# The first y tile of an output projection: loaded into raw weight buffers, and its two casts put behind the last V strip's copies on ScalarE

## The chip, the core and the metric

The kernel runs on one core of a Trainium2 chip. The metric is device time in microseconds (us) of one execution, lower is better. Engines are named as the profile names them: PE (TensorE, matmuls), PEld (its weight loads), DVE (VectorE), ACT (ScalarE), POOL (GpSimd) and SPq (SyncE's queue, which issues all DMAs here).

## The reference

One encoder layer, applied to a prompt of 1024 tokens and a sample of 256, each with 16 meta tokens ahead, in float32:

```python
u = rms_norm(h, norm_w) @ w_in                      # 2048 -> 6656
qa, ka, va, za, qb, kb, vb, zb = split(u)
ya = global_gqa(rope(norm(qa)), rope(norm(ka)), va) * silu(za)          # 8 heads, 2 KV heads
yb = neighbourhood_attention(norm(qb), norm(kb), vb, rpb) * silu(zb)    # 8 heads, windows of 8 x 16
y = concat([ya, yb]) @ w_out
return h + y                                        # meta tokens dropped
```

## The kernel before

Activations lie transposed: model dimension on the 128 partitions, tokens along the free axis. Tokens are taken in two chunks (`chunk1`, `chunk2`). In each, the input projection runs strip by strip, a strip being 128 output columns (one head of Q, K, V or Z). `strips` (L192) walks the 2048 input dimensions in four chunks of four 128-row tiles (`WCH` = 4): it loads 256 KB of weights into a tile `wr` of the pool `raw` and calls `split` (L64). Nearly all large products are float32 done as three passes over a high and a low part: `split` has ScalarE cast a tile to the high part (L66) and VectorE subtract it to get the low part (L67). The three matmuls per tile are L227 to L229; results gather in the PSUM tiles `pp`, one of 512 tokens (operand `x`) and one of 272 (operand `xb`).

The pools that matter here: `raw` has 3 buffers in chunk 2, `w` has 4 buffers for high parts (tag `wh`) and 4 for low parts (tag `wl`). A raw buffer comes free when VectorE has made the low part from it, a wh or wl buffer only when TensorE has done the matmuls that read it.

Chunk 2 ends with the V strip of the last local head and then its Z strip (`self.turn` is set there: in each weight chunk the 272 tokens come first). A V strip is scaled by VectorE (`v_rows`, L289, tile `vt`), transposed by TensorE into the one PSUM tile of the pool `tp` (L540), and copied out by ScalarE (`rows_out`, L542 and L547, tile `vl`), from which it is stored. For the last V strip the transposes and the copies fall into the Z strip behind it: first a `tp` tile of 512 tokens, then one of 272, whose copies are an L542 of 128x256 and an L547 of 16x128.

Then comes the output projection (`outproj`, L1095): seven products of half matrices (numbered 1, 2, 5, 6, 7, 3, 4 in `order`, a scheme with seven instead of eight), each over 5 token tiles, for two column halves `b`. One such step is 24 matmuls (L1056, L1057, L1058: y high by w high, y high by w low, y low by w high, for k = 0 to 7). The very first step puts its result into the `tp` tile (`products`, `first`), so it can only begin when the last V copies have emptied that. Its operands are 16 weight tiles `wm` (`w_load`, `w_operand`; loaded into `ww` tiles that take over the buffers of `xb`, and split into `wm` tiles that take over those of `x`), and the y tile (1, 0) in two halves of four k each. `y_load` (L975) loads a half straight into a wl buffer, where VectorE makes the low part in place; `y_operand` (L989) casts the high part `yh`. Between the first steps stand pieces of the last local head's attention (`attend_strip`: scores L485, values L516 and L519 for four column strips), entered by a list of due work.

The order on each engine comes from a scheduler, with edges set by hand: `place_after` keeps an instruction behind another on the same engine. `behind_v` (L1034) puts a split's subtraction behind the last V scaling, and its cast behind one of the last two 512- or 256-wide V copies (`vlcopies`): behind the one but last, until more than 8 weight tiles have been made.

Of the kernel before, what the change touches and what calls it, by code (L numbers as in the profile page):

```python
# [12 lines left out]
F32 = mybir.dt.float32  # L13
F32R = mybir.dt.float32r
# [7 lines left out]
P = 128  # L22
# [26 lines left out]
WCH = 4  # L49
# [10 lines left out]
class Kern:  # L60
# [914 lines left out]
    def y_load(self, p, t):  # L975

        def half(i, h):
            r = self.yr.tile([P, 8, P], F32, tag="yr", name="yr")
            self.nc.sync.dma_start(r[:], self.yd[i][:, NT * h + t])
            return r[:]  # L980

        if p in (1, 2):
            los = [self.w.tile([P, WCH, P], F32R, tag="wl", name="yl") for _ in range(2)]
            for i, l in enumerate(los):
                self.lasty = self.nc.sync.dma_start(l[:].bitcast(F32), self.yd[p - 1][:, t, WCH * i:WCH * i + WCH]).ins
            return los
        return [half(*x) for x in {7: [(0, 0), (0, 1)], 5: [(0, 1), (1, 1)], 6: [(0, 0)], 3: [(1, 0)], 4: [(1, 1)]}[p]]

    def y_operand(self, p, t, r):  # L989
        nc = self.nc  # L990
        if p in (1, 2):
            his, los, full = [], r, [l[:].bitcast(F32) for l in r]
            for l, f in zip(los, full):
                his.append(self.w.tile([P, WCH, P], F32R, tag="wh", name="yh"))
                i = self.split(his[-1][:], l[:], f)
                if (p, t) == (1, 0):
                    self.behind_v(i)
            return his, los
        if p == 4:
            v = r[0]  # L1000
        elif p == 7:
            v = r[0]
            nc.vector.tensor_tensor(out=v, in0=v, in1=r[1], op=ALU.subtract)
        else:
            v = self.ysum[t][:]
            a, b, op = {5: (r[0], r[-1], ALU.add), 6: (v, r[0], ALU.subtract), 3: (r[0], v, ALU.subtract)}[p]
            nc.vector.tensor_tensor(out=v, in0=a, in1=b, op=op)
        his, los = [], []
        for i in range(2):
            his.append(self.w.tile([P, WCH, P], F32R, tag="wh", name="yh"))  # L1010
            los.append(self.w.tile([P, WCH, P], F32R, tag="wl", name="yl"))
            self.split(his[i][:], los[i][:], v[:, WCH * i:WCH * i + WCH])
        return his, los
# [318 lines left out]
```

## Time and profile before

| what | value |
|---|---|
| time, median of 3 runs | 2164.05 us (2163.06 to 2164.53) |
| span of the profiled execution | 2164.5 us, the same as the slowest run's time |
| TensorE busy | 2154.5 us |
| VectorE, ScalarE, GpSimd busy | 1654.7, 1187.6, 524.2 us |
| DMA queues' share of 16 engines | 53.7% |
| first matmul of the output projection | 1766.4 us |

In a time line each row is start, duration, engine, line, operation, output and input, and in brackets the idle time of that engine before the row and what ended it. A row with x4 holds four instructions, and its duration runs from the first's start to the last's end. Operations of one engine overlap a little, so the distance between two starts is shorter than one duration. A row of waits is: who, for whom, us in total, times, the longest. The granted clock is TensorE's, 1.00 being full speed.

### The profile page before, as it was taken

The page shows a single profiled execution, that of the slowest core. Times are in us where ns is not written, and L with a number is a line of the kernel's source. Part 1 is how long each engine was busy: PE and PEld are TensorE (multiplying, and loading weights), DVE is VectorE, ACT ScalarE, POOL GpSimd, SP SyncE. Part 2 cuts the span into 40 slices and gives each one's busy share as a digit, 9 for nine tenths or more (in the row PEclk, how much of TensorE's full clock was granted, in tenths as well). Part 3 has the DMA queues.
Part 4 walks back from the last instruction along what each step waited for, and adds up shares of the span by engine and source line. Part 5 has one row for each costly group of instructions (what it writes and reads, how often), then busy time and mean ns, then how long its engine had stood idle before and what let it go on. Part 6 is the DMA issues. An engine that isn't in the chain of part 4 may idle for free.

```text
span 2164.5 us, 33971 instructions
## 1 busy us (share of the span) xinstructions
PE 2154.5 (100%) x11745; PEld 1879.5 (87%) x11745; DVE 1654.7 (76%) x2989; ACT 1187.6 (55%) x2411; POOL 524.2 (24%) x250
## 2 busy tenths in 40 slices
PE   9999999999999999999999999999999999999999
PEld 7888888888888999999999999998999988888887
DVE  7698976788874899996798988778787766545763
ACT  7677644554565777776677775444444454232230
POOL 1142422222221223231133224333333311000000
PEclk9999999999999999999999999999999999999999
DMA  8667789988654333324233244644433354662663
GB/s 295 215 190 221 239 298 313 340 282 266 211 187 137 95 101 107 110 96 141 92 109 102 93 126 158 184 151 142 137 123 122 119 190 150 238 231 95 233 224 107
DMA packets 257420, 377.24 MB, mean 174 GB/s; under 512 B 43072, under 2 KB 108768, under 8 KB 257248
## 3 DMA queue, kind: packets, MB, share of 16 engines
q1 hardware_dynamic: 257248, 375.07, 53.7%
q8 instruction: 92, 1.51, 0.3%
q14 instruction: 80, 0.66, 0.1%
HBM read 281.01 MB, written 100.38 MB: 176 GB/s over the span
## 4 chain that ended last, share of the span: by engine, by line
PE 98%; DMA 1%; DVE 1%; SPq 0%; ACT 0%; issue 0%; DVEq 0%; ACTq 0%
PE pp L227 22%; PE pp L229 22%; PE pp L228 22%; PE pq L1056 6%; PE pq L1058 6%; PE pq L1057 6%; PE po L519 2%; PE sp L485 2%; PE sp L378 1%; PE sp L379 1%; PE sp L377 1%; PE po L420 1%; PE po L419 1%; PE po L418 1%; PE tp L540 0%; DMA yl<-yd 0%
## 5 line engine op out<-in xcount | busy, mean ns | idle before, releaser
L227 PE MATMUL pp<-x,wh 128*128 128x512 f32 (+1 forms) x1664 | 655.2, 395 | 0.9 <-ACT wh L66 0.6
L229 PE MATMUL pp<-x,wl 128*128 128x512 f32 (+1 forms) x1664 | 647.6, 390 | 0.0
L228 PE MATMUL pp<-x,wh 128*128 128x512 f32 (+1 forms) x1664 | 647.1, 389 | 0.0
L229 PEld LDWEIGHTS pp<-x,wl 128*128 128x128 f32 x1664 | 312.4, 188 | 60.9 <-DVE wl L67 0.2
L227 PEld LDWEIGHTS pp<-x,wh 128*128 128x128 f32 x1664 | 312.4, 188 | 59.2 <-ACT wh L66 2.8
L228 PEld LDWEIGHTS pp<-x,wh 128*128 128x128 f32 x1664 | 312.9, 188 | 52.0
L262 POOL PARTITION_ALL_REDUCE m<-ms x78 | 222.7, 2855 | 356.1 <-ACT ms L260 295.6
L67 DVE TENSOR_TENSOR wl<-wr,wh 128x512 fp32r<-128x512 f32 (+2 forms) x287 | 212.9, 743 | 121.8 <-ACT wh L66 88.8
L346 POOL PARTITION_ALL_REDUCE tot<-a x80 | 180.6, 2258 | 439.0 <-DVE a L343 408.4
L66 ACT CAST wh<-wr 128x512 fp32r<-128x512 f32 (+2 forms) x287 | 173.7, 611 | 183.6 <-PE pp L228 170.3
L228 PE MATMUL pp<-xb,wh 128*128 128x272 f32 x832 | 240.7, 289 | 0.0
L227 PE MATMUL pp<-xb,wh 128*128 128x272 f32 x832 | 239.8, 288 | 0.0
L229 PE MATMUL pp<-xb,wl 128*128 128x272 f32 x832 | 239.1, 287 | 0.0
L328 POOL PARTITION_ALL_REDUCE ma<-m x80 | 114.3, 1428 | 452.4 <-DVE m L326 443.7
L1056 PE MATMUL pq<-wm,yh 128*128 128x512 f32 x560 | 219.7, 392 | 3.8 <-ACT vl L547 3.8
L1057 PE MATMUL pq<-wm,yh 128*128 128x512 f32 x560 | 219.4, 392 | 0.0
L1058 PE MATMUL pq<-wm,yl 128*128 128x512 f32 x560 | 219.1, 391 | 0.0
L227 PEld LDWEIGHTS pp<-xb,wh 128*128 128x128 f32 x832 | 156.5, 188 | 7.5
L228 PEld LDWEIGHTS pp<-xb,wh 128*128 128x128 f32 x832 | 156.5, 188 | 7.5
L229 PEld LDWEIGHTS pp<-xb,wl 128*128 128x128 f32 x832 | 157.4, 189 | 0.3
L1056 PEld LDWEIGHTS pq<-wm,yh 128*128 128x128 f32 x560 | 105.8, 189 | 26.0 <-ACT vl L547 4.2
L1058 PEld LDWEIGHTS pq<-wm,yl 128*128 128x128 f32 x560 | 105.8, 189 | 22.2
(212 smaller groups left out, 3927.5 us busy)
## 6 DMA issues: line engine op xcount, KB each, us to landing
wr<-in_w_in SPq DMA_DIRECT2D x413, 256.0 KB, 3.5
wld<-wl SPq DMA_DIRECT2D x132, 256.0 KB, 4.2
wl<-wld SPq DMA_DIRECT2D x132, 256.0 KB, 3.1
yr<-yd SPq DMA_DIRECT2D x35, 512.0 KB, 5.0
wq<-in_w_out SPq DMA_DIRECT2D x64, 256.0 KB, 5.0
td<-wq SPq DMA_DIRECT2D x64, 256.0 KB, 4.4
ww<-td SPq DMA_DIRECT2D x64, 256.0 KB, 5.2
ww<-in_w_out SPq DMA_DIRECT2D x48, 256.0 KB, 5.1
```

The source lines that it names most:

```text
L66: self.hi = nc.scalar.copy(hi, full).ins
L67: return nc.vector.tensor_tensor(out=lo, in0=full, in1=hi.bitcast(F32), op=ALU.subtract).ins
L227: nc.tensor.matmul(p[:, :n], wh[:, k, :], xh[:, :n], start=first, stop=False)
L228: nc.tensor.matmul(p[:, :n], wh[:, k, :], xl[:, :n], start=False, stop=False)
L229: self.lastmm = nc.tensor.matmul(p[:, :n], wl[:, k, :], xh[:, :n], start=False, stop=last).ins
L262: nc.gpsimd.partition_all_reduce(m2[:], ms[:], P, RED.add)
L328: nc.gpsimd.partition_all_reduce(ma[:], m1[:], P, RED.max)
L346: nc.gpsimd.partition_all_reduce(tot[:], a1[:], P, RED.add)
L485: nc.tensor.matmul(dst, k[:, o:o + P], qfv[:, a:e, :], start=True, stop=True)
L1056: nc.tensor.matmul(ps, yh, wh, start=k == 0, stop=False)
L1057: nc.tensor.matmul(ps, yh, wl, start=False, stop=False)
L1058: self.lastmm = nc.tensor.matmul(ps, yl, wh, start=False, stop=k == 7).ins
```

## The change

The first y tile, (1, 0), is no longer loaded into wl buffers but as float32 into two buffers of the pool `raw` (tiles `yf`). `y_operand` then makes both parts in new wh and wl buffers, and places the cast of half n behind `vlcopies[n - 2]`: the first half's behind the copy of 512 tokens, the second's behind the last 256-wide copy. The other tiles keep the old way; `behind_v` is still used for weight tiles.

```diff
+        if (p, t) == (1, 0):
+            out = [self.raw.tile([P, WCH, P], F32, tag="raw", name="yf") for _ in range(2)]
+            for i, f in enumerate(out):
+                self.lasty = self.nc.sync.dma_start(f[:], self.yd[0][:, 0, WCH * i:WCH * i + WCH]).ins
+            return out
         if p in (1, 2):
             los = [self.w.tile([P, WCH, P], F32R, tag="wl", name="yl") for _ in range(2)]
...
     def y_operand(self, p, t, r):
         nc = self.nc
+        if (p, t) == (1, 0):
+            his, los = [], []
+            for n, f in enumerate(r):
+                his.append(self.w.tile([P, WCH, P], F32R, tag="wh", name="yh"))
+                los.append(self.w.tile([P, WCH, P], F32R, tag="wl", name="yl"))
+                i = self.split(his[n][:], los[n][:], f[:])
+                self.place_after(i, self.lastvt, "drain first")
+                self.place_after(self.hi, self.vlcopies[n - 2], "drain first")
+            return his, los
         if p in (1, 2):
             his, los, full = [], r, [l[:].bitcast(F32) for l in r]
             for l, f in zip(los, full):
                 his.append(self.w.tile([P, WCH, P], F32R, tag="wh", name="yh"))
-                i = self.split(his[-1][:], l[:], f)
-                if (p, t) == (1, 0):
-                    self.behind_v(i)
+                self.split(his[-1][:], l[:], f)
             return his, los
```

ScalarE at the end of the last Z strip, before (`vl` copies of V, `yh` casts of y, `wm` casts of projection weights):

```order
L542 COPY vl<-tp 128x512
L66 CAST yh<-yl 128x512
L66 CAST wm<-ww 128x512 x4
L66 CAST yh<-yl 128x512
L542 COPY vl<-tp 128x256
L547 COPY vl<-tp 16x128
L66 CAST wm<-ww 128x512 x4
```

The same place on ScalarE now:

```order
L542 COPY vl<-tp 128x512
L66 CAST yh<-yf 128x512
L66 CAST wm<-ww 128x512 x4
L542 COPY vl<-tp 128x256
L547 COPY vl<-tp 16x128
L66 CAST yh<-yf 128x512
L66 CAST wm<-ww 128x512 x4
L66 CAST yh<-yl 128x512
```

The second half's cast has gone from ahead of the last V copies to behind them, and a cast of tile (1, 1) has moved up behind the third group of weights.

VectorE at the same place, before (`yl` low parts of y, `wm` low parts of weights, `vt` and `z` the scaled last blocks of V and Z):

```order
L289 TENSOR_TENSOR vt<-pp,rb_320 128x272
L67 TENSOR_TENSOR yl<-yl,yh 128x512
L67 TENSOR_TENSOR wm<-ww,wm 128x512 x4
L67 TENSOR_TENSOR yl<-yl,yh 128x512
L302 TENSOR_TENSOR z<-pp,rb_320 128x272
L67 TENSOR_TENSOR wm<-ww,wm 128x512 x8
```

VectorE now:

```order
L289 TENSOR_TENSOR vt<-pp,rb_320 128x272
L67 TENSOR_TENSOR wm<-ww,wm 128x512 x4
L67 TENSOR_TENSOR yl<-yf,yh 128x512
L302 TENSOR_TENSOR z<-pp,rb_320 128x272
L67 TENSOR_TENSOR wm<-ww,wm 128x512 x4
L67 TENSOR_TENSOR yl<-yl,yh 128x512
L67 TENSOR_TENSOR yl<-yf,yh 128x512
L67 TENSOR_TENSOR wm<-ww,wm 128x512 x3
```

The first half's low part now stands behind the second four weights, and the second half's (the second `yl<-yf`) behind the third four and behind a low part of tile (1, 1). These two write wl buffers of the Z strip's third and fourth weight chunk; the loads of tile (1, 1) take those of the first and second.

SyncE now issues the two loads of `yf` on either side of a store (`q2d`, L283) and a load (`qfull`, L866) of the last local head, ahead of the projection's first weight loads; where the loads of tile (1, 0) stood among the weight loads, there now stand those of tile (1, 1). On TensorE the order differs only in the steps behind: the values of the last head's first strip (L516) stand behind 24 matmuls of the third step, where they stood behind those and 6 of the fourth.

## The prediction

> **What bounds the kernel now.** I read the page's busy times and the chain first, then TensorE's waits, then the time lines of the engines round the one wait that stands out.
>
> ```profile
> PE 2154.5 (100%) x11745; PEld 1879.5 (87%) x11745; DVE 1654.7 (76%) x2989; ACT 1187.6 (55%) x2411; POOL 524.2 (24%) x250
> PE 98%; DMA 1%; DVE 1%; SPq 0%; ACT 0%; issue 0%; DVEq 0%; ACTq 0%
> PE pq L1056 <- ACT vl L547: 3.8, 1, 3.8
> PE pp L227 <- ACT wh L66: 0.6, 1, 0.6
> ```
>
> TensorE is the bound: 2154.5 of 2164.5 us busy, and 98% of the chain. No edit on another engine pays except where TensorE waits, and it has one wait worth having: 3.8 us before the first product of the output projection (L1056). TensorE's time line at that place, then windows of the same trace (us of the stretch; busy time and count of PE, PEld, DVE, ACT, POOL; granted clock; DMA share; GB/s):
>
> ```profile
> 1762.19 0.39 PE L229 MATMUL pp<-x,wl 128*128 128x512 f32 x1
> 1766.38 0.79 PE L1056 MATMUL pq<-wm,yh 128*128 128x512 f32 x1 [3.80 <-ACT vl L547]
> 1774.84 0.60 PE L485 MATMUL sp<-qfull,kfull 128*128 128x128 f32 x4
> 1776.04 0.53 PE L1056 MATMUL pq<-wm,yh 128*128 128x512 f32 x1
> 1781.63 0.61 PE L485 MATMUL sp<-qfull,kfull 128*128 128x128 f32 x4
> ...
> 5.00:8.00 3.00, 2.48 (x9) 1.60 (x10) 2.45 (x6) 2.05 (x7) 0.00 (x0) 1.00 0.84 236
> 1762.50:1766.40 3.90, 0.10 (x2) 0.02 (x1) 0.46 (x1) 1.11 (x4) 0.00 (x0) 0.92 1.09 372
> 1766.40:1769.00 2.60, 2.60 (x6) 2.12 (x7) 2.60 (x6) 2.60 (x6) 0.00 (x0) 0.50 1.00 347
> 1769.00:1772.00 3.00, 3.00 (x8) 2.32 (x8) 3.00 (x6) 3.00 (x8) 0.00 (x0) 0.50 0.48 140
> ```
>
> The first product (24 matmuls) takes 1766.38 to 1774.84, 8.46 us; the second, the same 24, takes 1776.04 to 1781.63, 5.59 us, 0.23 a matmul. The windows say why: the granted clock is 0.50 for most of the first product. So the wait costs twice: without it the first product could start at 1762.19 + 0.23 = 1762.42; it starts 3.96 us later and then loses 8.46 - 5.5 = 2.96 us to the half clock. At most 6.9 us are to be had, 0.32%. (About 0.2%, 4.3 us, is what a measurement of this kernel can tell from no change.)
>
> Who holds TensorE? ScalarE (ACT), SyncE's queue (SPq) and VectorE (DVE) at that place:
>
> ```profile
> 1754.80 0.58 ACT L542 COPY vl<-tp 128x512 f32<-128x512 f32 x1
> 1758.49 0.62 ACT L66 CAST yh<-yl 128x512 fp32r<-128x512 f32 x1 [3.11 <-DMA yl<-yd]
> 1761.13 0.62 ACT L66 CAST wm<-ww 128x512 fp32r<-128x512 f32 x1 [0.34 <-DMA ww<-in_w_out]
> 1765.29 0.62 ACT L66 CAST yh<-yl 128x512 fp32r<-128x512 f32 x1 [3.53 <-DMA yl<-yd]
> 1765.81 0.36 ACT L542 COPY vl<-tp 128x256 f32<-128x256 f32 x1
> 1766.08 0.25 ACT L547 COPY vl<-tp 16x128 f32<-16x128 f32 x1
> ...
> 1754.37 0.33 SPq L1023 DMA_DIRECT2D ww<-in_w_out  x1
> 1754.79 0.38 SPq L985 DMA_DIRECT2D yl<-yd  x1
> 1759.47 0.33 SPq L985 DMA_DIRECT2D yl<-yd  x1
> ...
> 1753.66 2.49 DVE L67 TENSOR_TENSOR wm<-ww,wm 128x512 fp32r<-128x512 f32 x4
> 1761.79 0.69 DVE L67 TENSOR_TENSOR wm<-ww,wm 128x512 fp32r<-128x512 f32 x1 [0.15 <-ACT wm L66]
> 1766.55 0.43 DVE L302 TENSOR_TENSOR z<-pp,rb 128x272 f32<-128x272 f32 x1
> 1766.90 4.95 DVE L67 TENSOR_TENSOR wm<-ww,wm 128x512 fp32r<-128x512 f32 x8
> ```
>
> ScalarE stands 3.53 us before the second half of the first y tile, whose load was issued only at 1759.47; behind that cast wait the last V copies, which empty the PSUM tile (tp) that the first product needs. The load is late because its buffer is a wl buffer of the last strip and because SyncE issues it behind twelve weight loads.
>
> **The change part by part.** *The loads.* Each half now needs a raw buffer, freed when VectorE has split the last strip's second and third weight chunk:
>
> ```profile
> 1740.41 0.68 DVE L67 TENSOR_TENSOR wl<-wr,wh 128x512 fp32r<-128x512 f32 x1
> 1744.54 0.67 DVE L67 TENSOR_TENSOR wl<-wr,wh 128x512 fp32r<-128x512 f32 x1
> 1743.65 0.32 SPq L283 DMA_DIRECT2D q2d<-rs_r  x1
> 1746.55 0.32 SPq L866 DMA_DIRECT2D qfull<-q2d  x1
> 1750.04 1.05 ACT L66 CAST q<-qfull 128x1024 fp32r<-128x1024 f32 x1 [2.27 <-DMA vm<-vmd]
> ww<-in_w_out SPq DMA_DIRECT2D x16, 256.0 KB, 5.0
> ```
>
> The first load goes out at 1740.41 + 0.68 = 1741.1, ahead of a store that SyncE issues at 1743.65 anyway: free. The second stands behind qfull's load, at about 1746.9; even at the 5.0 us that a weight load of the same size takes to land, it is there by 1752. Both halves are in SBUF before ScalarE wants them (1754.80 + 0.58 = 1755.4). That takes the 3.11 and the 3.53 us out of ScalarE's queue. The price is one more issue and 256 KB in front of qfull's arrival and the first four weight loads: 262 kB at the 372 GB/s of the window above is 0.70 us. Those casts have some air, as VectorE starts its four wm subtractions at 1753.66 behind q's; but q's own cast (1750.04) can move too. The fifth weight load (1754.37) waits for the first of those subtractions, 1753.66 + 0.68, and everything behind it on SyncE follows. I call its delay s: 0 if the air covers it, 0.7 if nothing does; I take 0.3, since only q's load shares its arrival with the new one. The loads of tile (1,1) take the old places and bytes of tile (1,0)'s among the weight loads, so nothing else moves there.
>
> *ScalarE.* Ahead of the last V copies there now stand four wm casts and no y cast that can wait. The last of the four waited for its weights until 1761.13 before. It will again, to 1761.13 + s; behind a 512-wide cast the next operation starts 0.52 later (1765.29 to 1765.81), the next 0.27 later, and the last takes 0.25: the copies end at 1762.17 + s = 1762.5. TensorE could start at 1762.42. So the old wait is gone but for 0.1 us.
>
> *What is late next: VectorE.* The first half's yl now stands behind the four subtractions of wm: the fourth starts at 1761.79 + s = 1762.1, yl 0.61 later (the pitch in the row of eight: (4.95 - 0.69)/7), 1762.7, and ends at 1763.4. The third matmul needs it as weights, and a weight load takes 0.19 (188 ns, the page's row below): it starts at 1763.6, not 1762.9. The second half's yl stands behind z (0.35, 1766.55 to 1766.90), four more wm, and a yl of tile (1,1): it starts at 1762.7 + 0.61 + 0.35 + 4 x 0.61 + 0.61 = 1766.7, ends at 1767.4, and the fifteenth matmul, its first reader, runs at 1767.6 instead of 1763.6 + 12 x 0.23 = 1766.4.
>
> ```profile
> L1058 PEld LDWEIGHTS pq<-wm,yl 128*128 128x128 f32 x560 | 105.8, 189 | 22.2
> ```
>
> *The clock.* Two waits remain, about 0.8 and 1.2 us. In 1762.50:1766.40 the clock averages 0.92, so it fell to half (1 - 0.92)/0.5 x 3.9 = 0.6 us before the end, over 3 us after the last matmul; a wait of 0.6 us (L227, the second row of waits) in 5.00:8.00 left it at 1.00. I take full clock, between 0 and 2.96 us lost, near the 0 since 1.2 is closer to 0.6 than to 3.8. [...] The windows show half clock from 1766.4 to past 1772, so the measured 2.96 stands.
>
> *The sum.* From the fifteenth matmul ten remain, 2.3 us: the scores (L485) start at 1767.6 + 2.3 = 1769.9, against 1774.84. Gain 4.9 us (5.2 for s = 0, 4.5 for s = 0.7). Downstream TensorE has no wait in the old trace, and what feeds it there is released by TensorE itself, so I expect the gain to reach the end. The profiled span is 2164.5, equal to the slowest of the three runs (2164.53) and 0.45 above the median: so the new span is 2159.6 and the new median 2164.05 - 4.9 = 2159.15, or 2159.2.
>
> **The rivals.** *The weights stay late (0.18).* The early loads are 512 KB; if both push the saturated weight loads by their full 0.70 us, and the last four of the eight wm arrive later than ScalarE comes to them, s grows to 1.4 or beyond and each us is lost one for one: gain 2.5 to 4, 2160 to 2161.6. For it: the 1.09 DMA share in 1762.50:1766.40. Against: the first load flies while SyncE idles.
>
> *Short waits throttle too (0.06).* Two waits of 2 us together within 5 us might halve the clock as one long one does. Price: the 2.96 us again, gain 1.9, 2162.1. Against: 5.00:8.00, TensorE busy 2.48 of 3.00 at clock 1.00. [...]
>
> *A new wait in the attention behind it: slower (0.05).*
>
> ```profile
> 1779.10 0.33 SPq L985 DMA_DIRECT2D yl<-yd  x1
> 1782.17 0.62 ACT L66 CAST yh<-yl 128x512 fp32r<-128x512 f32 x1 [3.49 <-DMA yl<-yd]
> 1787.20 0.41 DVE L338 TENSOR_TENSOR Pm<-Sm,Pm 16x256 fp32r<-16x256 f32 x1
> 1790.37 0.28 PE L516 MATMUL po<-Pm,vm 128*128 128x256 f32 x1
> ```
>
> The cast of tile (1,2) waits 3.49 us for its load, ahead of the exponentials whose result (Pm, 1787.20 + 0.41) the values matmul L516 takes at 1790.37: 2.8 us of air. In the new order L516 comes six matmuls earlier, leaving 2.8 - 1.4 = 1.4. To turn the change into a loss this place must eat 4.9 us: a wait of over 3 us, which halves the clock and costs 2.96 more. That needs the load to land 1.4 + 3.3 = 4.7 us later than its 3.1 (1779.10 to 1782.17); then 3.3 + 2.96 - 4.9 = 1.4 us slower, 2165.4. Against: 5.0 us is the median of the weight loads in the crowd, not 7.8.
>
> *The change doesn't do what it says (0.04).* If the raw buffers came free as late as the wl buffers did, the y cast would wait as before: 2164. The two rows of wl<-wr speak against it.
>
> *No wait at all (0.03).* If the weights land earlier and VectorE keeps pace, up to 6.9 us: 2157.2.
>
> **How the numbers follow.** The forecast has 0.64, the rivals 0.18, 0.06, 0.05, 0.04 and 0.03. The forecast's own range is 2158.6 to 2160.0 (s from 0 to 0.7, with the runs' scatter of 0.3 at the ends). With the late weights and the short-wait clock the range is 2158.3 to 2162.2, leaving out the slower case, the change that does nothing, the last rival, and the misses of those inside. The 0.2% bound lies at 2159.7, inside the forecast's range: I give 0.51 of its 0.64 to the faster side, 0.04 of the late weights and 0.03 of the last rival: 0.58. Slower is 0.05, with 0.37 within 0.2%.
>
> **What would show it right or wrong.** In the changed profile: y casts on ScalarE without a wait for a DMA; the first L1056 within half a us of the last strip's matmul; TensorE waits of about 0.7 and 1.2 us for VectorE's L67 in the third and fifteenth matmul of that product; granted clock 1.00 there; the first scores near 1769.9, and no TensorE wait behind. It is wrong if the wait for ScalarE stays, if the clock still falls to 0.50, or if L516 waits.

## The result and the profile after

| | before | after |
|---|---|---|
| time, median of 14 runs each | 2164.62 us (2163.06 to 2166.25) | 2160.49 us (2159.27 to 2160.92) |
| ratio | | 0.9981, 95% interval 0.9973 to 0.9988 |
| span of the profiled execution | 2164.5 us | 2157.5 us |
| that execution's own time | about 2166.3 us (worked out: its span and 1.77) | 2159.27 us (measured) |
| mean granted clock, each kernel's profile | 0.998 | 1.000 |

The change gains 4.1 us, 0.19%; 4.9 us and a median of 2159.2 had been forecast. 2160.49 lies above the forecast's own range (2158.6 to 2160.0) and inside the one that takes in its rivals (2158.3 to 2162.2).

The own time of a profiled execution lies some 1.77 us above its span (2159.27 and 2157.5 here, 2162.48 and 2160.7, 2163.97 and 2162.2 in two later profiles of before; over all runs 1.73 to 2.0). So the profile of before was not a run near the median: its span of 2164.5 makes a time of about 2166.3, which among the fourteen only the longest, 2166.25, comes near. The profile of after was the shortest of its fourteen. The two profiles differ by 7.0 us, the medians by 4.1.

The busy times and the chain of the page of after, and then the two largest rows of TensorE's waits (who, for whom, us in total, times, the longest):

```profile
PE 2151.3 (100%) x11745; PEld 1877.5 (87%) x11745; DVE 1658.5 (77%) x2989; ACT 1189.0 (55%) x2411; POOL 522.3 (24%) x250
PE 99%; DMA 0%; DVE 0%; SPq 0%; issue 0%; ACT 0%
```

```profile
PE warm L633 <- DVE wz L630: 1.2, 1, 1.2
PE pp L227 <- ACT wh L66: 0.9, 2, 0.6
```

The larger is the program's start. The 3.8 us before the first product are gone, and no wait has taken their place. TensorE's time line at the place (L1068 to L1070 are the old L1056 to L1058), with a window over the first product (us of the stretch; busy time and count of PE, PEld, DVE, ACT, POOL; granted clock; DMA share; GB/s):

```profile
1762.15 0.39 PE L229 MATMUL pp<-x,wl 128*128 128x512 f32 x1
1762.38 0.39 PE L1068 MATMUL pq<-wm,yh 128*128 128x512 f32 x1
...
1765.55 0.39 PE L1070 MATMUL pq<-wm,yl 128*128 128x512 f32 x1
...
1767.82 0.60 PE L485 MATMUL sp<-qfull,kfull 128*128 128x128 f32 x4
```

```profile
1762.40:1767.80 5.40, 5.40 (x25) 4.48 (x24) 4.60 (x9) 4.16 (x10) 0.00 (x0) 1.00 0.59 209
```

The first product follows the Z strip at once, at full clock, and takes 5.44 us; the scores start at 1767.82 where they started at 1774.84, 7.02 us sooner, which is the whole difference of the two spans (7.0 us). The fifteenth matmul, for which 1.2 us of waiting had been forecast, runs at 1765.55 without any. ScalarE, VectorE and SyncE's queue show why:

```profile
1754.23 0.62 ACT L66 CAST yh<-yf 128x512 fp32r<-128x512 f32 x1
1758.41 0.62 ACT L66 CAST wm<-ww 128x512 fp32r<-128x512 f32 x1 [0.56 <-DMA ww<-in_w_out]
1758.94 0.37 ACT L542 COPY vl<-tp 128x256 f32<-128x256 f32 x1
1759.20 0.25 ACT L547 COPY vl<-tp 16x128 f32<-16x128 f32 x1
```

```profile
1759.67 0.69 DVE L67 TENSOR_TENSOR yl<-yf,yh 128x512 fp32r<-128x512 f32 x1
...
1763.73 0.69 DVE L67 TENSOR_TENSOR yl<-yf,yh 128x512 fp32r<-128x512 f32 x1
```

```profile
1739.76 0.32 SPq L985 DMA_DIRECT2D yf<-yd  x1
...
1744.56 0.42 SPq L985 DMA_DIRECT2D yf<-yd  x1
```

Both loads go out some 15 us before their casts, and the first cast (1754.23) doesn't wait for its load; nor does the second, at 1759.36. The last of the second four weight casts, forecast for 1761.13 + 0.3, runs at 1758.41, and the V copies end at 1759.45, 2.9 us before TensorE is done with the Z strip. So VectorE too is early: the second yl ends at 1764.42, 1.1 us before its reader.

### The profile page after: what moved, and what is told of

Read it like the earlier page. It is cut to its first block, busy times and chain, and to the rows that moved or that the text cites. A ratio compares the mean times of both kernels' runs of the same rounds, so it can differ in the third digit from the quotient of the medians.

```text
span 2157.5 us, 33972 instructions
## 1 busy us (share of the span) xinstructions
PE 2151.3 (100%) x11745; PEld 1877.5 (87%) x11745; DVE 1658.5 (77%) x2989; ACT 1189.0 (55%) x2411; POOL 522.3 (24%) x250
## 4 chain that ended last, share of the span: by engine, by line
PE 99%; DMA 0%; DVE 0%; SPq 0%; issue 0%; ACT 0%
PE pp L227 22%; PE pp L229 22%; PE pp L228 22%; PE pq L1069 6%; PE pq L1068 6%; PE pq L1070 6%; PE po L519 2%; PE sp L485 2%; PE sp L378 1%; PE sp L379 1%; PE sp L377 1%; PE po L420 1%; PE po L419 1%; PE po L418 1%; PE tp L540 0%; PE sp L430 0%
## 5 line engine op out<-in xcount | busy, mean ns | idle before, releaser
L1068 PE MATMUL pq<-wm,yh 128*128 128x512 f32 x560 | 218.3, 390 | 0.0
L1070 PE MATMUL pq<-wm,yl 128*128 128x512 f32 x560 | 218.2, 390 | 0.0
L1068 PEld LDWEIGHTS pq<-wm,yh 128*128 128x128 f32 x560 | 105.1, 188 | 21.8
L1070 PEld LDWEIGHTS pq<-wm,yl 128*128 128x128 f32 x560 | 105.1, 188 | 21.8
```

What stands on the lines that cost most here:

```text
L1068: nc.tensor.matmul(ps, yh, wh, start=k == 0, stop=False)
L1070: self.lastmm = nc.tensor.matmul(ps, yl, wh, start=False, stop=k == 7).ins
```

## The experiments

The letters A and B stand in each quoted expectation for the theories that it names there. "Before" with a ratio is the kernel before, run on the same chip in the same series: its medians were 2164.8 us (33 runs), 2164.37 us (23) and 2164.53 us (13).

### Both kernels profiled again

Both were run again as they are. Their profiles are counted with those above as the first of each kernel.

> The kernel before once more, for a second profile of it. The two theories: A, the wait before the output projection differs from execution to execution (it hangs on how late ScalarE and the loads come out of the last head's work), and the profile that the forecast was made from had a long one. Then this profile shows a wait for L547 shorter than 3.8 us or a shorter stretch at half clock, together about 4 us instead of 6.9, and a span near 2163. B, the wait is always 3.8 us and the changed kernel loses elsewhere what it should have won: then 3.8 us again, half clock for 6 us, a span of 2164.5. Time against itself: ratio 1.000.

> The changed kernel once more, for a second profile. Theory A: TensorE again has no wait at the first product, or at most some tenths of a us for L67 of VectorE at its third or fifteenth matmul; span 2157.5 to 2159. Theory B: the first profile was lucky, and waits of 0.8 and 1.2 us for VectorE, as forecast, stand there now; span 2158.7 to 2159.5. Ratio to before 0.998 in both.

Measured: before 2164.3 us (11 runs, 2162.48 to 2165.6), ratio 0.9999 (0.9990 to 1.0008); after 2160.32 us (2159.43 to 2161.32), ratio 0.9980 (0.9971 to 0.9988). The place in the new profile of before (span 2160.7):

```profile
1761.79 0.39 PE L229 MATMUL pp<-x,wl 128*128 128x512 f32 x1
1765.42 0.50 PE L1056 MATMUL pq<-wm,yh 128*128 128x512 f32 x1 [3.25 <-ACT vl L547]
...
1771.00 0.61 PE L485 MATMUL sp<-qfull,kfull 128*128 128x128 f32 x4
```

The wait is there and hardly shorter, but the first product takes 5.58 us, at full clock throughout (1.00 from 1765.40 to 1771.00): the scores start 3.2 us after those of the changed kernel's first profile, not 7.0. So the price varies from execution to execution, as theory A has it, and is not B's fixed 6.9 us; A's own sizes (about 4 us, a span near 2163) were missed too, at 3.5 us and 2160.7. In the second profile of after (span 2157.6) TensorE waits only 0.23 us for VectorE, at the fifteenth matmul: theory A there as well.

> The kernel before, a third look. Theory A (the clock is decided in fixed stretches of about 3.4 us that run free of the program): the wait for ScalarE is again 3.1 to 3.9 us, and the half clock behind it lasts 0, about 3.4 or about 6.8 us, nothing between; with 0 the span is near 2160.7, with 3.4 near 2162.5, with 6.8 near 2164. Theory B (half clock grows smoothly with the wait): its length lies anywhere between 0 and 6.8.

This execution took 2163.97 us, near before's median. TensorE's rows, and windows of the clock (us of the stretch, busy time and count of PE, PEld, DVE, ACT and POOL, then the clock):

```profile
1761.83 0.39 PE L229 MATMUL pp<-x,wl 128*128 128x512 f32 x1
1765.30 0.50 PE L1056 MATMUL pq<-wm,yh 128*128 128x512 f32 x1 [3.08 <-ACT vl L547]
...
1772.49 0.60 PE L485 MATMUL sp<-qfull,kfull 128*128 128x128 f32 x4
```

```profile
1763.16:1766.57 3.41, 1.27 (x6) 1.05 (x7) 1.71 (x4) 2.36 (x6) 0.00 (x0) 1.00 1.08 393
1766.50:1766.60 0.10, 0.10 (x2) 0.06 (x2) 0.10 (x1) 0.10 (x1) 0.00 (x0) 0.84 0.85 328
1766.60:1769.90 3.30, 3.30 (x9) 2.62 (x8) 3.30 (x6) 3.30 (x8) 0.00 (x0) 0.50 0.63 211
1769.90:1770.00 0.10, 0.10 (x2) 0.04 (x1) 0.10 (x1) 0.10 (x2) 0.00 (x0) 0.59 0.79 113
```

The clock is 1.00 before and 0.50 behind the window of 0.84 over 0.10 us, so this was at half clock for its last 0.03 us: half clock runs from 1766.57 to 1769.98, 3.41 us. It began 1.27 us after TensorE had gone back to work. The first product took 7.19 us, 1.75 more than the 5.44 at full clock. In the first profile of before, windows narrowed in the same way:

```profile
1765.70:1765.76 0.06, 0.00 (x0) 0.00 (x0) 0.00 (x0) 0.06 (x1) 0.00 (x0) 0.98 1.03 384
...
1765.82:1772.50 6.68, 6.12 (x14) 4.79 (x15) 6.56 (x12) 6.67 (x16) 0.00 (x0) 0.50 0.78 259
1772.50:1772.60 0.10, 0.10 (x2) 0.08 (x1) 0.10 (x1) 0.00 (x0) 0.00 (x0) 0.57 1.11 318
```

Half clock from 1765.76 to 1772.59: 6.83 us, twice 3.41. Theory A holds here: 0, 3.41 and 6.83 us in the second, third and first profile, after waits of 3.25, 3.08 and 3.80 us. The half clock began 3.34 us after the end of the Z strip in the first profile, with TensorE still idle, and 4.51 us after it in the third: it is not TensorE's stop that sets where a stretch begins. The 33 runs of before in the first of these series fall into three kinds by their mean clock: 4 kept 1.000 (2162.25 to 2163.12 us), 18 show 0.999 (2163.54 to 2166.27), 11 show 0.998 (2165.41 to 2166.91).

On the side of the changed kernel, what parted its typical runs from its two profiled ones, which were both the shortest of their series?

> The changed kernel, a third look. Theory A: where its time is near the median (2160.4) or above, TensorE shows a wait for VectorE's yl of about 1 us at the third or fifteenth matmul of the first product. Theory B: such a wait is 0 to 0.3 us whatever the time, and a run that is 1 us longer has its last Z matmul 1 us later.

> The changed kernel, a fourth look, for the same question: theory A has a wait of about 1 us for VectorE's yl in a run near 2160.4, theory B has 0 to 0.3 us and a later last Z matmul.

They took 2160.31 and 2160.7 us, near the median. TensorE's one new wait in the third profile, as a row of the waits:

```profile
PE pq L1070 <- DVE yl L67: 0.6, 1, 0.6
```

VectorE in the fourth profile, and TensorE there, with the same wait in brackets:

```profile
1762.03 0.68 DVE L67 TENSOR_TENSOR yl<-yf,yh 128x512 fp32r<-128x512 f32 x1
1762.98 2.60 DVE L67 TENSOR_TENSOR wm<-ww,wm 128x512 fp32r<-128x512 f32 x4
1765.50 0.69 DVE L67 TENSOR_TENSOR yl<-yl,yh 128x512 fp32r<-128x512 f32 x1
1766.10 0.69 DVE L67 TENSOR_TENSOR yl<-yf,yh 128x512 fp32r<-128x512 f32 x1
```

```profile
1762.17 0.39 PE L229 MATMUL pp<-x,wl 128*128 128x512 f32 x1
1766.84 0.50 PE L1070 MATMUL pq<-wm,yl 128*128 128x512 f32 x1 [1.04 <-DVE yl L67]
1769.25 0.60 PE L485 MATMUL sp<-qfull,kfull 128*128 128x128 f32 x4
```

This is the chain that had been forecast: the second yl stands behind four weight subtractions and one of the next tile's, ends at 1766.79, and the fifteenth matmul is the first that needs it. The wait is 0, 0.23, 0.60 and 1.04 us in the four profiles, at 2159.27, 2159.43, 2160.31 and 2160.7 us: theory A. Theory B is not borne out: the last Z matmul starts at 1762.15 in the first profile and at 1762.17 in the fourth, 1.4 us apart in time. The product takes 5.44, 5.98, 6.38 and 6.86 us, so that a wait costs some 0.3 to 0.4 us more than the wait listed.

What makes VectorE late in these two is the weights: the chain that ends at this matmul goes back through the subtractions and a cast of `wm` to a weight load, landed at 1760.42 in the third profile and at 1764.21 in the fourth.

### The two halves of the change

Raw buffers and early loads alone, with the casts where `behind_v` puts them (against the changed kernel):

```diff
-                self.place_after(i, self.lastvt, "drain first")
-                self.place_after(self.hi, self.vlcopies[n - 2], "drain first")
+                self.behind_v(i)
```

> Only the raw buffers: the loads are early, the casts keep the old placing, so both y casts and one of tile (1,1) stand ahead of the last V copies. If the late load was the whole wait (theory A), ScalarE has nothing to wait for there but two casts of 0.52 us more ahead of the copies, which its lead covers: time as the changed kernel's, within 1 us. If the order of the casts is what counts, the time stays near before's, over 2 us above the changed kernel's.

Measured: 2161.27 us (2160.28 to 2163.64, 11 runs), ratio 0.9985 (0.9976 to 0.9994). That is theory A: the median lies 1 us above the changed kernel's. In its profile no wait is left before the first product, but VectorE makes a yl of the next tile early (at 1761.07) and the second yl of this one late, behind five weight subtractions, the last of which had to wait for its weights. The row of VectorE and the row of waits:

```profile
1765.54 0.68 DVE L67 TENSOR_TENSOR yl<-yf,yh 128x512 fp32r<-128x512 f32 x1
```

```profile
PE pq L1069 <- DVE yl L67: 1.1, 1, 1.1
```

Two of its eleven runs show a clock of 0.999 (2163.57 and 2163.64 us); what they waited for wasn't profiled.

The order alone: the loads go into wl buffers as late as before, and only the cast of half n is placed as in the change (against before).

```diff
-                    self.behind_v(i)
+                    self.place_after(i, self.lastvt, "drain first")
+                    self.place_after(self.hi, self.vlcopies[n - 2], "drain first")
```

> Only the order: loads stay late in wl buffers, the second half's cast stands behind the last V copies. The first product starts on time but its fifteenth matmul waits for the second half's load, cast and subtraction. From the first profile of before: landing 1765.2, cast to 1765.9, subtraction to 1766.6, so a wait of 0.6 us or less there and no half clock: 1 us above the changed kernel at most. If the early loads are what counts, the wait for L547 goes over to the fifteenth matmul in full, 3 us or more, and half of the gain is lost.

Measured: 2160.15 us (2158.91 to 2161.49, 11 runs), ratio 0.9979 (0.9970 to 0.9988), the same as the whole change within the intervals. Its profile is of the longest of its eleven runs. ScalarE there:

```profile
1762.90 0.25 ACT L547 COPY vl<-tp 16x128 f32<-16x128 f32 x1
1766.17 0.62 ACT L66 CAST yh<-yl 128x512 fp32r<-128x512 f32 x1 [3.02 <-DMA yl<-yd]
```

and TensorE, with the first matmul of the product, which follows the Z strip at once, and the thirteenth, the first that reads the second half:

```profile
1763.70 0.39 PE L1057 MATMUL pq<-wm,yh 128*128 128x512 f32 x1
...
1766.84 0.50 PE L1057 MATMUL pq<-wm,yh 128*128 128x512 f32 x1 [0.26 <-ACT yh L66]
```

ScalarE still stands 3 us before the late load, but nobody that TensorE needs stands behind that cast any more, and the half itself isn't read before the thirteenth matmul: a wait of 0.26 us is listed there, and the product takes 6.27 us, 0.8 more than in the profile after. The two parts are two cures for one wait, so their gains do not add.

### The clock apart from the wait

The kernel before, with eight matmuls that nobody reads laid into the wait:

```diff
         if first:
+            d, z = self.sp.tile([P, 2, QB], F32, tag="sp", name="warm")[:].rearrange("p a b -> p (a b)"), self.lastmm
+            for _ in range(8):
+                i = nc.tensor.matmul(d, ws[0][:, 0, :P], ws[0][:, 0, :], start=True, stop=True).ins
+                self.place_after(i, z, "warm")
```

(with an edge that keeps the first product behind them).

> The kernel before with eight matmuls that nobody reads (warm<-wm, 0.23 us each, 1.8 us in all) between the Z strip's last matmul and the first product. They lie inside TensorE's wait (3.25 us in the second profile of before, 3.80 in the first), so they take no time of their own and change nothing on ScalarE. Theory A (the wait is paid twice, once as a wait and once as half clock, and the clock falls only where TensorE is idle for a whole stretch of about 3.4 us): the wait is cut to 1.4 to 2.0 us behind the eight, the granted clock stays 1.000 in every run, and the time is that of those runs of before that kept 1.000, 2162.3 to 2163.1: about 2162.5, 2 us below before's median, with the runs closer together. Theory B (the wait is the whole cost and the clock a by-product of how the profile counts): no change, 2164.5.

Measured: 2163.11 us (2161.36 to 2165.12, 11 runs), ratio 0.9994 (0.9985 to 1.0003). Ten of its eleven runs kept a clock of 1.000, where 4 of 23 runs of before did beside it. In its profile TensorE waits 0.7 us behind the eight:

```profile
1761.62 1.98 PE L1052 MATMUL warm<-wm 128*128 128x512 f32 x8
1764.31 0.50 PE L1060 MATMUL pq<-wm,yh 128*128 128x512 f32 x1 [0.72 <-ACT vl L547]
1769.91 0.60 PE L485 MATMUL sp<-qfull,kfull 128*128 128x128 f32 x4
```

The product takes 5.60 us though ScalarE is still late. So the half clock comes from TensorE standing idle, though in one run (2165.12 us, clock 0.999) it still fell. That it falls only behind a wholly idle stretch, as A had it, is not shown: in the third profile of before TensorE had worked 1.27 of the 3.41 us ahead of the fall. The gain in time, 1.3 us by the medians, is smaller than the 2 us that A expected, and the ratio's interval takes in 1: in time alone theory B is not ruled out.

### How much room the V copies have

The changed kernel, with ScalarE copies that nobody reads ahead of the last V copies, once with 12 and once with 24 (one of them lands behind the first V copy, the rest at the place):

```diff
+            late = self.t.tile([P, QB], F32, tag="t", name="late")
+            for _ in range(12):
+                i = nc.scalar.copy(late[:], self.rb[:, :QB]).ins
+                self.place_after(i, self.vlcopies[-2], "late")
+            self.place_after(self.vlcopies[-1], i, "late")
```

> The changed kernel with twelve ScalarE copies that nobody reads (128x256, some 0.3 us each), eleven of them just ahead of the last V copies: 11 x 0.31 = 3.4 us of delay there. Theory A (the V copies end 1.4 to 2.9 us before TensorE wants them, as the two profiles of the changed kernel show, 1760.62 against 1761.99 and 1759.45 against 1762.38): the first product waits 0.5 to 2.0 us, the clock stays 1.000, and the time is 2161 to 2162.5. Theory B (the forecast's: no slack, the copies end 0.1 us too late): all 3.4 us are added, 2163.9, and some runs lose clock besides.

> The same with twenty-four such copies, 23 x 0.31 = 7.1 us of delay. Slack of 1.4 to 2.9 taken off, the first product waits 4.2 to 5.7 us. Theory A (a whole idle stretch of about 3.4 us halves the clock, and it comes back after one or two such stretches): the clock falls in every run, mean 0.998 to 0.999, and the first product loses another 1.7 to 3.4 us: 2166.5 to 2169.5, so that twice the delay costs some four times as much as in the run with twelve. Theory B (waits cost their own length): 2164.6 to 2166.1.

Measured: 2165.22 us with 12 (2164.41 to 2166.43, 11 runs), ratio 1.0005 (0.9996 to 1.0014); 2170.61 us with 24 (2170.12 to 2171.62, 7 runs), ratio 1.0028 (1.0017 to 1.0039). Neither theory had the numbers, since the copies took more than the 0.31 us supposed, and the clock fell in all 18 runs (0.997 to 0.999). ScalarE and TensorE with 12:

```profile
1760.87 4.77 ACT L1000 COPY late<-rb 128x256 f32<-128x256 f32 x11
```

```profile
1762.59 0.39 PE L229 MATMUL pp<-x,wl 128*128 128x512 f32 x1
1766.11 0.80 PE L1073 MATMUL pq<-wm,yh 128*128 128x512 f32 x1 [3.13 <-ACT vl L547]
1773.19 0.60 PE L485 MATMUL sp<-qfull,kfull 128*128 128x128 f32 x4
```

The eleven took 4.77 us, 0.43 each. Without them the V copies would have started at 1760.87 and ended near 1761.4 (by the 0.26 from 1758.94 to 1759.20 and the 0.25 after it, in the profile after), 1.4 us before TensorE is done with the Z strip (1762.59 + 0.23): the room is A's, and not B's 0.1 us too little. The product then takes 7.08 us, 1.6 more than at full clock. With 24 (23 at the place, 9.99 us), TensorE:

```profile
1761.94 0.39 PE L229 MATMUL pp<-x,wl 128*128 128x512 f32 x1
1771.82 0.79 PE L1073 MATMUL pq<-wm,yh 128*128 128x512 f32 x1 [9.50 <-ACT vl L547]
1779.67 0.60 PE L485 MATMUL sp<-qfull,kfull 128*128 128x128 f32 x4
```

The span, 2169.3, is 11.8 us over that of the profile of after: 9.50 of wait, and 7.85 - 5.44 = 2.4 of half clock (together 11.9; the Z strip ended a little earlier). Here, too, the wait is paid with its clock.

### The second half's low part ahead

The changed kernel, with VectorE's second yl ahead of the weight subtractions that it stood behind:

```diff
                 self.place_after(self.hi, self.vlcopies[n - 2], "drain first")
+            self.ylo = i
...
-                self.split(his[-1][:], l[:], f)
+                i = self.split(his[-1][:], l[:], f)
+                if (p, t) == (1, 1):
+                    self.place_after(i, self.ylo, "y first")
...
+        if 9 <= self.wouts <= 16:
+            self.place_after(i, self.ylo, "y first")
```

> The changed kernel with VectorE's second yl subtraction of the first y tile put ahead of four weight subtractions and one of the next tile's, so that it is ready some 3 us earlier (in the second profile of the changed kernel it ran at 1764.81 and the fifteenth matmul waited 0.23 us for it). Theory A (the forecast's term of 0.8 + 1.2 us of waits for VectorE is there in the typical run, and the two profiles of the changed kernel, both the fastest of their series at 2159.27 and 2159.43, missed it): the typical run gains 0.7 to 1.2 us on the changed kernel's 2160.4, so 2159.2 to 2159.7, and the runs come closer together. Theory B (VectorE costs the changed kernel nothing or 0.2 us also in a typical run, and what parts its runs lies ahead of this place): 2160.2 to 2160.5, scattered as before.

Measured: 2159.19 us (2158.91 to 2160.65, 9 runs), ratio 0.9977 (0.9967 to 0.9987). VectorE there:

```profile
1761.90 0.69 DVE L67 TENSOR_TENSOR yl<-yf,yh 128x512 fp32r<-128x512 f32 x1
...
1762.86 0.68 DVE L67 TENSOR_TENSOR yl<-yf,yh 128x512 fp32r<-128x512 f32 x1
1763.45 2.49 DVE L67 TENSOR_TENSOR wm<-ww,wm 128x512 fp32r<-128x512 f32 x4
```

The V copies are as late as in the third and fourth profiles (ended at 1761.68), and no wait of TensorE is listed in the product. It takes 5.68 us, and the scores start at 1767.76; the 0.24 us over 5.44 lie at the third matmul, which reads the first yl (ended at 1762.59). The wait at the fifteenth matmul is gone, as theory A has it, and the median lies 1.2 us under the changed kernel's 2160.4. That size is not shown: the two were not timed against each other, both ratios are to before, and their intervals overlap. On this chip the changed kernel's two single runs (2160.31 and 2160.7) lie above eight of the nine. That the runs come closer together, which A also had, did not happen: they span 1.7 us, the changed kernel's 1.7 and 1.9. Its median is the lowest of the study.

## Why the prediction was right or wrong

- **The place and the cause: right.** TensorE's one wait worth having was the one for the last V copies, held by a y cast that waited for its load. It is gone in all four profiles of the changed kernel, and either half of the change removes it. Of the two reasons given for the late load, only the place behind twelve weight loads is borne out. The buffer is not: in the profile of before SyncE issued that load at 1759.47, as soon as a weight load had landed (1759.46), and no wait for the matmuls that free a wl buffer is listed there.
- **A wait paid twice: right in kind, mis-sized as a typical cost.** 3.96 and 2.96 us were read off one execution. The third profile of before, near the median, has 1765.30 - 1762.06 = 3.24 and 1.75 us, together 5.0 instead of 6.9; the second has 3.40 and 0.14. The half clock lasted 6.83 us in the first profile (TensorE worked from 1766.38 to 1772.59, 6.2 us, before the clock was back) and 3.41 us in the third; the second had none. So "the measured 2.96 stands" was true of its execution, and too dear for one near the median. Nor does each wait of over 3 us halve the clock, as the rival of a wait in the attention had it: 3.40 us idle left it at 1.00 in the second profile.
- **Span against time: wrong.** "equal to the slowest of the three runs (2164.53) and 0.45 above the median" took a span for a time. With the 1.77 us on top, the execution took about 2166.3, 1.6 us above the median of the fourteen runs and as long as the longest of them. A gain read off it could not be taken from the median.
- **The price of the early load (s of 0.3): not seen.** The last of the second four weight casts was to run at 1761.13 + 0.3; it ran at 1758.41 in the first profile, and the V copies ended at 1759.45, 1760.62, 1761.48 and 1761.80 in the four, 0.6 to 2.9 us before TensorE wanted them, where the sum had them 0.1 us late. The 1761.13 was itself late for this kernel: in the second and third profiles of before the same cast ran at 1759.82 and 1760.11. Whether the early load costs anything can't be seen under this scatter of some 2 us, and the bounds of s (0 to 0.7) left no room for it.
- **VectorE late next: right for the second half, wrong for the first.** The 0.8 us at the third matmul came in no profile of the changed kernel: in the fourth the first yl ended at 1762.71, in time. The 1.2 us at the fifteenth were 0, 0.23, 0.60 and 1.04 us, and the wait went when its order was mended.
- **The clock stays full behind the change: right.** All 27 runs of the changed kernel show 1.000.
- **The sum: near, and partly by luck.** Scores were forecast for 1769.9 and a gain of 4.9. They start at 1767.82, 1767.97, 1768.84 and 1769.25. From there to the end of the span it is 389.6 to 389.7 us in every profile on record, before, after and experiments alike. So the gain at the scores reaches the end, as was said: no wait stood behind. The median gain of 4.1 is some 5.0 taken away (third profile of before) less the 0.9 by which the product ran longer than 5.44 in the third profile of after. That 4.9 came close to it rests on two errors against each other: a base 2 us too dear, and 2.0 us of waits behind it where runs near the median have 0.9 to 1.4. The forecast time was 1.3 us too short, by 0.8 of gain and by 0.6 of base: before's median is 2164.62 in fourteen runs, and was 2164.05 in the first three.
- **The chances.** 0.58 were given to a gain of over 0.2%; 0.19% fell just short of it.
- **The rivals.** No wait at all (6.9 us) is what the first pair of profiles shows, and not what the medians do. A clock that falls over short waits and a new wait in the attention are in no profile of the changed kernel: behind waits of 0.23, 0.60 and 1.04 us the clock of the whole execution was 1.000. Late weights never held the V copies long enough there to stop TensorE; they do reach it through VectorE, as the chains of the third and fourth profiles show.

What stays open: why the weight loads, and with them ScalarE, come up to 2.4 us earlier or later at this place from one execution of a kernel to the next (ends of the V copies, above). No run here varied that.

## What to carry over

Before a gain is read off one profile, set that execution's own time beside the median: a wait that starts a clock fall has a price that changes from run to run (0.14, 1.75 and 2.96 us on top of waits of 3.25, 3.08 and 3.80 us here). A cast that waits for its load (3.53 us here) harms by what stands behind it in its engine's queue; putting it behind them cured this as well as loading early did (2160.15 and 2161.27 us). And when the long wait goes, ask which engine is late next and reorder that one too: here that took away a wait of up to 1.04 us.

## What the runs showed of the hardware

- The half clock came in stretches of 3.41 us: one (third profile of before), two (6.83, first profile), and with 24 late copies three:

```profile
1766.40:1766.60 0.20, 0.00 (x0) 0.00 (x0) 0.00 (x0) 0.17 (x2) 0.00 (x0) 0.67 0.13 51
1766.60:1776.60 10.00, 4.78 (x11) 3.80 (x12) 4.28 (x8) 9.68 (x23) 0.00 (x0) 0.50 0.22 66
1776.60:1776.80 0.20, 0.20 (x2) 0.12 (x1) 0.20 (x2) 0.20 (x2) 0.00 (x0) 0.73 1.05 312
```

  from 1766.47 to 1776.71, 10.24 us; it began 4.30 us after the end of the Z strip, and TensorE stood idle until 1771.82.
- In the 3.41 us ahead of the fall TensorE had worked 1.27 us (37%, the first window of the third profile of before). The clock was not back 3.41 us after its fall in the first profile, at 1769.17, though TensorE had worked from 1766.38 on, 2.79 us (82%). An idle time of 3.40 us (second profile) cost no clock at all; one of 3.24 us (third) was followed by 3.41 us of half clock, which cost 1.75 us. What decides between these was not measured.
- Eleven and 23 ScalarE copies of 128x256 in a row into one tile took 0.43 us each. The single such copy behind the first V copy, with the same source and tile, took 0.41 us and let the next ScalarE instruction, which writes elsewhere, start after 0.31 us (1755.11 to 1755.42, the run with 12). So the copies in a row did not overlap; that it is the shared tile that keeps them apart is not shown.
